# Two of four 31-tap convolution chunks taken off VectorE, six blocks ahead of the mixers' norm, and a last norm in smaller pieces

## The chip, the cores and the metric

The kernel runs on one core of a Trainium2 chip. The metric is the device time of one execution in microseconds (us), as the median of several. The engines are called by the names of the profile: PE is TensorE (PEld its weight loads), DVE is VectorE, ACT is ScalarE, POOL is GpSimd, and SP issues the DMAs.

## What is computed

A sequence of 256 tokens with 1024 features runs through two layers of a first block and two layers of a second block. The second block is where the change lies. A layer of it is: a SwiGLU feed-forward network (FFN), a layer norm, a mixer of three branches, a norm, a second FFN, a norm.

```python
h = layer_norm(ALPHA * h + 0.5 * swiglu(h, ffn1...), ln1)
mix = hybrid_mixer(h, ...)      # gated delta rule + convolution branch + latent attention, gated, @ w_out
h = layer_norm(ALPHA * h + mix, ln2)
h = layer_norm(ALPHA * h + 0.5 * swiglu(h, ffn2...), ln3)

def conv_branch(u, ...):
    h = u[..., :512] * sigmoid(u[..., 512:])
    h = causal_depthwise_conv(h, dw_w) + dw_b     # 31 taps, 512 channels
    h = silu(layer_norm(h, ln_g, ln_b))
    return h @ w_pw2 + b_pw2
```

## The kernel before

Activations lie with 128 features on the partitions and the 256 tokens along the free dimension, so a vector of 1024 features is eight chunks of 128x256. Weights come from memory in blocks of 128x1024 float32. Each block is split into a high part (`whi`, a copy on ACT) and a rest (`wlo`, a subtraction on DVE), and each product is three matmuls: high by high, high by low, low by high (`mm3`, L513). Eight PSUM banks (`ps`), twelve places for split weights (`spl`) and ten places for tiles of up to 288 columns (`t1`) are shared by all stages (`ROOM`, L1775).

The order of the work is not that of the program text. Every instruction is first recorded as an `Op` with a price (`price`, L277) and with what it must wait for. A planner (`run`, L305, and `schedule`, L318) lays the whole list out six times, backwards and forwards, picks the line with the earliest end by its prices, and the instructions are issued in that order. On the chip each engine runs its own instructions strictly in that order. All recorded instructions are issued from L409, so all rows of the profile have that line, and they are told apart by their tiles. The prices know each engine by itself; they have no term for two engines that hinder each other. A POOL operation on two tensors is priced at 0.154 us plus its columns by 480 per us.

The parts that the change touches, all in the second block:

- `taps_slow` (L1587) is one 128-channel chunk of the 31-tap convolution on DVE: one product with a bias, then 30 multiply-and-adds into the sum `cv`, each of 256 columns, reading `gluu` at a shifting offset. `conv_chunk` (L1574) calls it for each of four chunks in each of two layers. The four sums first meet in `conv_norm` (L1595), and what comes of that is used late in the mixer, with the weights `w_pw2`.
- `second_first` (L1213) says which weight blocks are multiplied with the not yet normed features (tiles `r`) while the norm's statistics are being worked out (`begin`, L574). Their results hold PSUM banks until the norm's factors are there, and are then mended on DVE by `fix` (L1176): a copy of two columns and two operations of 256 columns, `fx`. FFNs begin with six such blocks, mixers with four: `wi_krab` and three of `wi_dn`. All later blocks multiply the normed features (tiles `h`).
- `normed_begin` (L1103) holds `done`, which adds each result chunk to `x`, and `end` (L1152). For the last norm of the kernel, `end` multiplies all of `x` by one factor and adds another, in pieces of two chunks on DVE, then scales each chunk on ACT and stores it.
- `ffn` (L710) gives its results in two halves that `done` adds one after the other.

Other work that matters to the steps below: `delta` (L1356) and `unit_inverse` (L1482) are the gated delta rule, a long chain of small matmuls (`sm`) with DVE, ACT and POOL steps between them; the tile `NQ` is masked on POOL in it. `rsqrt` (L615) works out the norms' factor `rstd` on POOL.

Of the kernel before, what the change touches and what calls it, by code (L numbers as in the profile page):

```python
# [12 lines left out]
ACTF = mybir.ActivationFunctionType  # L13
# [3 lines left out]
P = 128  # L17
# [394 lines left out]
class Net:  # L412
# [294 lines left out]
            return Feat(norm, pss, fix)  # L707
        return take, end

    def ffn(self, F, wg, wu, wd, done, wide=False):  # L710

        a = self.halves("a", KF)
        for j in range(KF):
            g, gb = self.lin(wg[j], F, wide)
            u, ub = self.lin(wu[j], F, wide)
            sg = self.t([P, T], "sg")
            self.nc.scalar.activation(out=sg, in_=g, func=ACTF.Silu, **({} if gb is None else {"bias": gb}))
            av = self.t([P, T], "av")
            self.times(av, u, ub, sg)
            self.cut(a[j], av)  # L720
        for m in range(KD):
            ps = self.linear_f([w[m] for w in wd], a, True)
            done(m, ps[:, 0], ps[:, 1])

    def new_x(self):
        self.x = self.kept([P, KD, T], "x")
# [376 lines left out]
    def normed_begin(self, x, scale, gb, last=False):  # L1103


        nc = self.nc
        st = {}
        raw = []

        def sums(m):  # L1110
            if m == 0:
                st["s1"] = self.t([P, T], "s1")
                nc.vector.tensor_copy(out=st["s1"], in_=x[m])
            else:
                nc.vector.tensor_tensor(out=st["s1"], in0=st["s1"], in1=x[m], op=ALU.add)
            st["s2"] = self.add_square(st.get("s2"), x[m])
            if not last:
                self.cut_raw(raw[m], x[m], self.col(gb, 2 * m), self.col(gb, 2 * m, 2))

        def done(m, ps, ps2=None):  # L1120
            if ps2 is not None and m >= 4:
                nc.vector.tensor_tensor(out=x[m], in0=x[m], in1=ps2, op=ALU.add)
            if m < 4:
                nc.vector.scalar_tensor_tensor(out=x[m], in0=x[m], scalar=ALPHA / scale, in1=ps, op0=ALU.mult, op1=ALU.add)
            else:
                nc.vector.tensor_tensor(out=x[m], in0=x[m], in1=ps, op=ALU.add)
            if ps2 is not None and m < 4:
                nc.vector.tensor_tensor(out=x[m], in0=x[m], in1=ps2, op=ALU.add)
            if m == 1:
                st["s0"] = self.t([P, T], "s0")  # L1130
                nc.vector.tensor_tensor(out=st["s0"], in0=x[0], in1=x[1], op=ALU.add)
            if m == 2:
                ps0 = self.token_sums([st["s0"]])
                mu = st["mu"] = self.t([P, NT], "mu0")
                nc.vector.tensor_scalar(out=mu, in0=ps0[:, 0, :], scalar1=1.0 / 256, scalar2=None, op0=ALU.mult)
            if m == 3:
                pb = self.spread(st["mu"])
                if not last:
                    raw[:] = self.halves("r", KD, W)
                for k in range(4, KD):  # L1140
                    nc.vector.scalar_tensor_tensor(out=x[k], in0=x[k], scalar=ALPHA / scale, in1=pb, op0=ALU.mult,
                                                   op1=ALU.subtract)
                for k in range(4):
                    nc.vector.tensor_tensor(out=x[k], in0=x[k], in1=pb, op=ALU.subtract)
                for k in range(2):
                    sums(k)
            elif m > 3:
                if m < 6:
                    sums(m - 2)
                sums(m)  # L1150

        def end(first):  # L1152
            if last:
                for z, cols in zip((ALU.mult, ALU.add), self.moments(st["s1"], st["s2"], D, 1e-5 / scale ** 2)):
                    by = self.spread(cols).unsqueeze(1).to_broadcast([P, 2, T])
                    for m in range(0, KD, 2):
                        nc.vector.tensor_tensor(out=self.x[:, m:m + 2], in0=self.x[:, m:m + 2], in1=by, op=z)
                for m in range(KD):
                    nc.scalar.activation(out=x[m], in_=x[m], func=ACTF.Identity, scale=self.col(gb, 2 * m),
                                         bias=self.col(gb, 2 * m + 1))  # L1160
                    nc.sync.dma_start(out=self.out[m], in_=x[m])
                return None
            pss = self.begin(first, raw)
            rn = self.t([P, 2, T], "rn")
            nc.scalar.copy(out=rn, in_=self.spread2(*self.moments(st["s1"], st["s2"], D, 1e-5 / scale ** 2)))
            norm = self.halves("h", KD)
            for m in range(KD):
                w = self.t([P, T], "lnw")
                nc.scalar.activation(out=w, in_=rn[:, 1], func=ACTF.Identity, scale=self.col(gb, 2 * m),
                                     bias=self.col(gb, 2 * m + 1))  # L1170
                nc.vector.scalar_tensor_tensor(out=x[m], in0=x[m], scalar=self.col(gb, 2 * m), in1=rn[:, 0],
                                               op0=ALU.mult, op1=ALU.mult)
                nc.vector.tensor_tensor(out=x[m], in0=x[m], in1=w, op=ALU.add)
                self.cut(norm[m], x[m])

            def fix(ps, M):  # L1176
                c = self.t([P, 2], "fc")
                nc.vector.tensor_copy(out=c[0:M], in_=ps[:, T:W])
                o = self.t([P, T], "fx")
                nc.vector.tensor_tensor(out=o[0:M], in0=ps[:, 0:T], in1=rn[0:M, 0], op=ALU.mult)  # L1180
                nc.vector.scalar_tensor_tensor(out=o[0:M], in0=rn[0:M, 1], scalar=c[0:M, 0:1], in1=o[0:M],
                                               op0=ALU.mult, op1=ALU.add)
                return o[0:M], c[0:M, 1:2]
            return Feat(norm, pss, fix)
        return done, end
# [27 lines left out]
    def second_first(self, l, i):  # L1213
        ins = self.ins
        if i == 2:
            return [ins["wi_krab"][l]] + [ins["wi_dn"][l, j] for j in (4, 5, 6)]
        g, u = ins[f"f{(i + 1) // 2}g"][l], ins[f"f{(i + 1) // 2}u"][l]
        return [g[0], u[0], g[1], u[1], g[2], u[2]]

    def second_layer(self, l, x, F, last):  # L1220
        ins = self.ins
        for i in (1, 2, 3):
            end_all = last and i == 3
            done, end = self.normed_begin(x, 1.0 if i == 2 else 0.5, f"ln{i}{l}", end_all)
            if i == 2:
                self.hybrid(l, F, done)
            else:
                k = (i + 1) // 2
                self.ffn(F, ins[f"f{k}g"][l], ins[f"f{k}u"][l], [ins[f"f{k}d{j}"][l] for j in range(3)], done,
                         True)  # L1230
            if l == 0 and i == 3 and self.single:
                return end([])
            nl, ni = (l, i + 1) if i < 3 else (l + 1, 1)
# [340 lines left out]
    def conv_chunk(self, l, j, pa, pg, c, cs):  # L1574
# [7 lines left out]
        nc.vector.memset(u[:, 0:N], 0.0)  # L1582
        nc.vector.scalar_tensor_tensor(out=u[:, N:], in0=sg, scalar=1.0, in1=a, op0=ALU.add, op1=ALU.mult)
        cs.append(c)
        self.taps_slow(c, u, f"dw{l}_", 31, j, self.col(f"dw_b{l}", j))

    def taps_slow(self, out, src, name, n, ch, bias):  # L1587
        nc = self.nc
# [347 lines left out]
```

## Time and profile before

| | |
|---|---|
| time, median of 3 runs | 2287.04 us (2286.8 to 2287.19) |
| time of the profiled execution | 2288.66 us |
| its span in the profile | 2286.9 us |
| PE busy | 2249.1 us, 98% |
| PEld busy | 2103.8 us, 92% |
| DVE busy | 1858.2 us, 81% |
| ACT busy | 1288.8 us, 56% |
| POOL busy | 50.5 us, 2% |

The span is the time from the first to the last recorded instruction or transfer of one profiled execution; 1.8 us of that execution lie outside it, and that execution took 1.6 us more than the median. A matmul's end is modelled in the trace, so a busy PE is read together with what is marked as its idle time, and with the granted clock.

### The profile page before, as it was taken

The numbers are of one execution on the slowest core, as the hardware profiler recorded it, in microseconds if no ns is written. First come the engines' busy times: TensorE is split into PE (matmuls) and PEld (weight loads), VectorE is DVE, ScalarE is ACT, GpSimd is POOL, SyncE is SP. The second block draws the span as 40 slices with busy tenths as digits, with TensorE's granted clock in tenths as the row PEclk, the third lists the DMA queues.
The fourth block names the chain that finished last, engine by engine and source line by source line (L and its number), as shares of the span: only waits on it lengthen the run. The fifth ranks groups of instructions, "written<-read, shape, count | busy, mean of one in ns | idle before, by whom it ended". The sixth has DMA issues, their size and how long they took to land.

```text
span 2286.9 us, 41903 instructions
## 1 busy us (share of the span) xinstructions
PE 2249.1 (98%) x15948; PEld 2103.8 (92%) x15948; DVE 1858.2 (81%) x3690; ACT 1288.8 (56%) x2328; POOL 50.5 (2%) x46
## 2 busy tenths in 40 slices
PE   7999999999999999999999999999999999999997
PEld 6998899999989999888899999988988899999886
DVE  8888998798789755777789979977876899969865
ACT  4444765455445554466474756654664674656652
POOL 0000100000000000000001000000000010000000
PEclk9999999999999999999999999999999999999998
DMA  8999469888787555755542356555555441555652
GB/s 329 336 323 320 133 233 317 272 275 296 270 299 238 184 186 182 247 191 183 187 149 67 129 168 203 202 183 186 188 190 178 137 165 55 186 165 194 204 180 87
DMA packets 139788, 469.81 MB, mean 205 GB/s; under 512 B 15681, under 2 KB 20801, under 8 KB 139586
## 3 DMA queue, kind: packets, MB, share of 16 engines
q1 hardware_dynamic: 139586, 467.13, 60.6%
q8 instruction: 125, 2.05, 0.4%
q14 instruction: 77, 0.63, 0.1%
HBM read 466.02 MB, written 1.05 MB: 204 GB/s over the span
## 4 chain that ended last, share of the span: by engine, by line
PE 87%; DVE 5%; DMA 5%; ACT 1%; issue 1%; POOL 0%; ACTq 0%; SPq 0%; POOLq 0%; DVEq 0%
PE mm L409 82%; PE sm L409 5%; DMA raw<-in_ffn_wd_dram 2%; DVE wlo L409 1%; DVE raw L409 1%; DMA raw<-in_w_ada_dram 1%; ACT whi L409 1%; DMA raw<-in_ffn_wg_dram 1%; DVE x L409 1%; DVE cv__22491 L409 0%; DVE NQ L409 0%; DMA raw<-in_ffn_wu_dram 0%; DMA raw<-in_w_out_dram 0%; POOL rstd L409 0%; DVE cv__14517 L409 0%
## 5 line engine op out<-in xcount | busy, mean ns | idle before, releaser
L409 ACT CAST whi<-raw 128x1024 fp32r<-128x1024 f32 (+3 forms) x796 | 778.7, 982 | 590.9 <-PE mm L409 289.7
L409 DVE TENSOR_TENSOR wlo<-raw,whi 128x1024 fp32r<-128x1024 f32 (+3 forms) x796 | 901.6, 1137 | 240.0 <-PE mm L409 194.9
L409 DVE CUSTOM_DVE_ANT_0 raw<-raw,crep 128x1024 f32<-128x1024 f32 x144 | 175.0, 1219 | 36.2 <-DMA raw<-in_w_ada_dram 35.6
L409 ACT COPY half<-mm 128x256 f32<-128x256 f32 x158 | 57.7, 367 | 38.9 <-PE mm L409 37.4
L409 DVE TENSOR_TENSOR half<-mm,half 128x256 f32<-128x256 f32 x158 | 66.4, 420 | 16.0 <-ACT half L409 14.9
L409 POOL TENSOR_TENSOR rstd<-var,constt 128x2 f32<-128x2 f32 x18 | 18.3, 1017 | 1995.2 <-DVE var L409 1959.7
L409 ACT ACTIVATE sq<-x 128x256 f32<-128x256 f32 x96 | 38.6, 411 | 42.0 <-DVE x L409 39.7
L409 ACT ACTIVATE sg<-mm 128x256 f32<-128x256 f32 x79 | 30.1, 382 | 41.8 <-PE mm L409 37.3
L409 ACT ACTIVATE sg<-half 128x256 f32<-128x256 f32 x79 | 32.9, 418 | 27.3 <-DVE half L409 26.2
L409 DVE SCALAR_TENSOR_TENSOR x<-mm,gate,x 128x256 f32<-128x256 f32 x88 | 41.3, 478 | 7.6 <-PE mm L409 7.5
L409 DVE TENSOR_TENSOR sq<-sq 128x256 f32<-128x256 f32 x89 | 37.2, 418 | 4.0 <-ACT sq L409 3.7
L409 DVE TENSOR_TENSOR av<-mm,sg 128x256 f32<-128x256 f32 x79 | 33.1, 419 | 8.4 <-PE mm L409 8.1
L409 DVE TENSOR_TENSOR x<-x,mm 128x256 f32<-128x256 f32 x56 | 23.3, 416 | 17.0 <-PE mm L409 16.8
L409 DVE TENSOR_TENSOR av<-half,sg 128x256 f32<-128x256 f32 x79 | 33.3, 423 | 2.0
L409 DVE SCALAR_TENSOR_TENSOR dnc<-dnu,colt,dnc 128x256 f32<-128x256 f32 x72 | 31.7, 477 | 3.7 <-ACT dnc L409 3.6
L409 DVE SCALAR_TENSOR_TENSOR cv__22491<-gluu,colt,cv__22491 128x256 f32<-128x256 f32 x60 | 29.9, 514 | 0.0
L409 DVE SCALAR_TENSOR_TENSOR cv__14517<-gluu,colt,cv__14517 128x256 f32<-128x256 f32 x60 | 28.9, 506 | 0.0
L409 DVE SCALAR_TENSOR_TENSOR cv__15244<-gluu,colt,cv__15244 128x256 f32<-128x256 f32 x60 | 26.5, 474 | 0.0
L409 DVE SCALAR_TENSOR_TENSOR cv__23214<-gluu,colt,cv__23214 128x256 f32<-128x256 f32 x60 | 26.4, 475 | 0.0
L409 PEld LDWEIGHTS sm<-invX,NQ 128*128 128x128 f32 x192 | 23.7, 192 | 2.0 <-issue 1.4
L409 PE MATMUL sm<-invX,NQ 128*128 128x64 f32 x192 | 24.4, 271 | 0.9 <-DVE invX L409 0.9
L409 ACT COPY invX<-sm 128x256 f32<-128x256 f32 x20 | 7.6, 378 | 30.0 <-PE sm L409 26.6
(3361 smaller groups left out, 7993.9 us busy)
## 6 DMA issues: line engine op xcount, KB each, us to landing
raw<-in_w_ada_dram SPq DMA_DIRECT2D x144, 512.0 KB, 5.2
raw<-in_ffn_wg_dram SPq DMA_DIRECT2D x88, 512.0 KB, 5.1
raw<-in_ffn_wu_dram SPq DMA_DIRECT2D x88, 512.0 KB, 4.9
raw<-in_ffn_wd_dram SPq DMA_DIRECT2D x64, 512.0 KB, 5.0
raw<-in_wi_gate_dram SPq DMA_DIRECT2D x48, 512.0 KB, 3.2
raw<-in_f1g_dram SPq DMA_DIRECT2D x44, 512.0 KB, 3.8
raw<-in_f1u_dram SPq DMA_DIRECT2D x44, 512.0 KB, 4.1
raw<-in_f2g_dram SPq DMA_DIRECT2D x44, 512.0 KB, 4.4
```

The lines of the kernel that those rows point to most:

```text
L409: fn(*[real(a) for a in args], **{k: real(v) for k, v in kw.items()})
```

## The change

- Chunks 0 and 1 of the four convolution chunks go through a new function, `taps_apart`: ACT makes each of the 31 products (the first with the bias, straight into the sum; the others into a tile `tap`), and POOL adds the 30 others to the sum, one after the other. Chunks 2 and 3 stay on DVE.
- The mixers' list in `second_first` gets two more blocks of `wi_dn`, numbers 7 and 0, so that six blocks run ahead of the norm.
- In the last norm, both factors are spread first, and then each piece of `x` is multiplied and added to before the next one; the first two pieces are single chunks, the other three are pairs.
- In the last FFN, the last result chunk is accumulated in one half (three matmuls of 256 columns instead of one of 512 and one of 256), so that `done` adds it once.

```diff
-    def ffn(self, F, wg, wu, wd, done, wide=False):
+    def ffn(self, F, wg, wu, wd, done, wide=False, last=False):
...
         for m in range(KD):
-            ps = self.linear_f([w[m] for w in wd], a, True)
-            done(m, ps[:, 0], ps[:, 1])
+            ps = self.linear_f([w[m] for w in wd], a, not last or m < KD - 1)
+            done(m, *([ps] if last and m == KD - 1 else [ps[:, 0], ps[:, 1]]))
...
             if last:
-                for z, cols in zip((ALU.mult, ALU.add), self.moments(st["s1"], st["s2"], D, 1e-5 / scale ** 2)):
-                    by = self.spread(cols).unsqueeze(1).to_broadcast([P, 2, T])
-                    for m in range(0, KD, 2):
-                        nc.vector.tensor_tensor(out=self.x[:, m:m + 2], in0=self.x[:, m:m + 2], in1=by, op=z)
+                by = [self.spread(cols) for cols in self.moments(st["s1"], st["s2"], D, 1e-5 / scale ** 2)]
+                for m, n in ((0, 1), (1, 1), (2, 2), (4, 2), (6, 2)):
+                    for r, op in zip(by, (ALU.mult, ALU.add)):
+                        nc.vector.tensor_tensor(out=self.x[:, m:m + n], in0=self.x[:, m:m + n],
+                                                in1=r.unsqueeze(1).to_broadcast([P, n, T]), op=op)
...
         if i == 2:
-            return [ins["wi_krab"][l]] + [ins["wi_dn"][l, j] for j in (4, 5, 6)]
+            return [ins["wi_krab"][l]] + [ins["wi_dn"][l, j] for j in (4, 5, 6, 7, 0)]
...
-        self.taps_slow(c, u, f"dw{l}_", 31, j, self.col(f"dw_b{l}", j))
+        (self.taps_apart if j < 2 else self.taps_slow)(c, u, f"dw{l}_", 31, j, self.col(f"dw_b{l}", j))
+
+    def taps_apart(self, out, src, name, n, ch, bias):
+
+        nc = self.nc
+        nc.scalar.activation(out=out, in_=src[:, 0:T], func=ACTF.Identity, scale=self.col(f"{name}0", ch), bias=bias)
+        for i in range(1, n):
+            p = self.t([P, T], "tap")
+            nc.scalar.activation(out=p, in_=src[:, i:i + T], func=ACTF.Copy, scale=self.col(f"{name}{i}", ch))
+            nc.gpsimd.tensor_tensor(out=out, in0=out, in1=p, op=ALU.add)
```

## Rows read from the trace of the kernel before

**Rows 1.** Busy time, share of the span and instructions of each engine, whole kernel.

```profile
PE 2249.1 (98%) x15948; PEld 2103.8 (92%) x15948; DVE 1858.2 (81%) x3690; ACT 1288.8 (56%) x2328; POOL 50.5 (2%) x46
```

**Rows 2.** Stretch, length; busy of PE, PEld, DVE, ACT, POOL; granted clock; DMA share, GB/s.

```profile
1197.00:1256.00 59.00, 58.05 (x487) 57.08 (x487) 55.99 (x133) 29.04 (x70) 8.09 (x5) 1.00 0.23 74
```

**Rows 3.** The same stretch, DVE instructions that touch `gluu` alone: length, DVE busy.

```profile
1197.00:1256.00 59.00, 26.80 (x60) 1.00 0.23 74
```

**Rows 4.** Timeline of PE, mixers' beginnings: start, duration, instruction [idle before, releaser].

```profile
1151.96 0.43 PE L409 MATMUL sm<-constt,rstd 128*128 128x128 f32 x2 [0.50 <-POOL rstd L409]
1160.01 0.58 PE L409 MATMUL mm<-h__13933,whi 128*128 128x256 f32 x1 [2.62 <-DVE h__13933 L409]
...
1809.35 0.43 PE L409 MATMUL sm<-constt,rstd 128*128 128x128 f32 x2 [0.49 <-POOL rstd L409]
1824.64 0.61 PE L409 MATMUL sm<-constt,krab__22127 8*128 8x8 f32 x4 [1.75 <-ACT krab__22127 L409]
1826.71 0.44 PE L409 MATMUL sm<-constt,dn__22130 128*128 128x128 f32 x2 [1.10 <-ACT dn__22130 L409]
```

**Rows 5.** Stretches just behind those waits, columns as in rows 2.

```profile
1160.00:1200.00 40.00, 39.99 (x315) 39.84 (x316) 36.37 (x89) 31.79 (x78) 0.00 (x0) 0.93 0.50 159
...
1800.00:1840.00 40.00, 36.65 (x289) 35.71 (x288) 35.50 (x84) 29.78 (x71) 1.75 (x1) 0.96 0.39 135
```

**Rows 6.** A FFN's beginning with six early blocks, columns as in rows 2.

```profile
1414.00:1445.00 31.00, 31.00 (x262) 31.00 (x261) 29.74 (x68) 19.81 (x36) 1.55 (x1) 1.00 0.58 199
```

**Rows 7.** One tile, first mixer: duration in ns (least/median/most), first and last start.

```profile
L409 DVE TENSOR_TENSOR fx<-mm,rn x4: 410/414/414, 1158.5 to 1164.9; 128x256 f32<-128x256 f32 x3, 72x256 f32<-72x256 f32 x1
```

**Rows 8.** Groups by shape, DVE taps in the two mixers: count, busy us, mean ns.

```profile
L409 DVE SCALAR_TENSOR_TENSOR cv__14517<-gluu,colt,cv__14517 128x256 f32<-128x256 f32 x60 | 28.9, 506 | 0.0
...
L409 DVE SCALAR_TENSOR_TENSOR cv__15244<-gluu,colt,cv__15244 128x256 f32<-128x256 f32 x60 | 26.5, 474 | 0.0
...
L409 DVE SCALAR_TENSOR_TENSOR cv__22491<-gluu,colt,cv__22491 128x256 f32<-128x256 f32 x60 | 29.9, 514 | 0.0
```

**Rows 9.** One tile, ACT products with a per-partition factor: durations as in rows 7.

```profile
L409 ACT ACTIVATE dnc<-dnu,colt x24: 495/508/551, 1161.7 to 1853.4; 128x256 f32<-128x256 f32 x24
```

**Rows 10.** One tile each, POOL's operations (the memset from the groups, with mean).

```profile
L409 POOL TENSOR_TENSOR NQ<-NQ,constt x8: 1092/1269/2013, 1227.9 to 1893.1; 128x512 f32<-128x512 f32 x8
L409 POOL TENSOR_TENSOR rstd<-var,constt x18: 695/709/1747, 13.9 to 2276.2; 128x2 f32<-128x2 f32 x18
L409 POOL MEMSET rope__67<- 64x256 f32 x2 | 0.6, 305 | 0.3 <-POOLq L1925 0.3
```

**Rows 11.** Timeline of POOL and DVE where both work, columns as in rows 4.

```profile
1227.93 2.33 POOL L409 TENSOR_TENSOR NQ<-NQ,constt 128x512 f32<-128x512 f32 x2 [11.23 <-DVE NQ L409]
1228.16 1.15 DVE L409 SCALAR_TENSOR_TENSOR cv__14517<-gluu,colt,cv__14517 128x256 f32<-128x256 f32 x1
...
1807.53 1.22 DVE L409 TENSOR_TENSOR wlo<-raw,whi 128x1024 fp32r<-128x1024 f32 x1
1807.55 1.75 POOL L409 TENSOR_TENSOR rstd<-var,constt 128x2 f32<-128x2 f32 x1 [186.17 <-DVE var L409]
```

**Rows 12.** Timeline of PE in the delta rule's chain, columns as in rows 4.

```profile
1234.14 1.08 PE L409 MATMUL sm<-invX,NQ 128*128 128x64 f32 x8 [0.93 <-DVE invX L409]
...
1896.67 0.55 PE L409 MATMUL sm<-invW,invY 128*128 128x64 f32 x3 [1.15 <-DVE invW L409]
```

**Rows 13.** Timeline of the kernel's last 15 us, columns as in rows 4.

```profile
2272.43 0.88 DVE L409 TENSOR_TENSOR x<-x,mm 128x256 f32<-128x256 f32 x2 [5.93 <-PE mm L409]
...
2277.68 1.88 DVE L409 TENSOR_TENSOR x<-x,sm 128x512 f32<-128x512 f32 x3 [0.59 <-PE sm L409]
2278.88 3.67 DVE L409 TENSOR_TENSOR x<-x,sm 128x512 f32<-128x512 f32 x6
2279.66 2.29 ACT L409 ACTIVATE x<-x,colt 128x256 f32<-128x256 f32 x4 [5.90 <-DVE x L409]
...
2282.05 2.07 ACT L409 ACTIVATE x<-x,colt 128x256 f32<-128x256 f32 x4
```

## What the change was predicted to do

> **What bounds the kernel now.** I began with the engines' busy times: PE is busy 2249.1 of 2286.9 us, DVE 81%, POOL 2% [rows 1]. The matmuls that the change leaves as they are fill the span, so an edit can only win time in which PE waits or runs at a lower clock. Next came the stretches: where the first mixer's convolution lies, DVE is busy 55.99 of 59 us, but PE 58.05 of the same 59 [rows 2]. DVE is full there because the planner fills its gaps with taps, which nobody waits for. Taps take 26.80 of the 55.99 [rows 3]. Last I read PE's timeline for waits in the three places that the diff touches: the mixers' beginnings [rows 4], the delta rule [rows 12] and the end [rows 13].
>
> **Six early blocks.** At the first mixer PE waits 0.50 us for the norm's factor and then 2.62 us for the first normed chunk `h`; at the second 0.49 us for the factor, 1.75 for `krab` and 1.10 for the first `dn` chunk [rows 4]. After each of these waits the granted clock is lower: 0.93 as a mean over 40 us and 0.96 [rows 5], so PE ran part of them at 1.2 instead of 2.4 GHz. That cost 40 x 0.07 = 2.8 and 40 x 0.04 = 1.6 us. The waits for `h`, `krab` and `dn` are 5.5 us, the clock 4.4, together 9.9; the two waits for the factor, 1.0 us more, come from POOL, which the edit leaves alone.
>
> Two more early blocks are work for PE that needs no normed chunk. A block is 8 x 3 = 24 matmuls; 262 of them, most of this size, take 31 us at the FFN's beginning [rows 6], so a block is some 2.8 us and two are 5.7 us, more than the longest wait. The cost is two more mendings on DVE, of two operations near 0.41 us and a small copy [rows 7]: about 2 us a layer, beside PE's 5.7. What is late next is the mendings themselves: `krab` is one of six and not of four. I leave half of its wait (0.9 us) standing and take -9.0 us, with the bounds -9.9 and 0. The weights of the two blocks are only issued earlier on SP's queue, behind the same 12 places. The nearest evidence that six are enough is that at an FFN, with six early blocks and the same norm, PE is busy 31.00 of 31.00 us at a clock of 1.00 [rows 6].
>
> **Taps on ACT and POOL.** Off DVE go 60 multiply-and-adds a layer, which hold it 26.5 us where nothing hinders them [rows 8]. As PE waits for DVE only here and there, this relief is worth at most the waits in the delta rule's chain, 0.93 and 1.15 us [rows 12]. ACT gets 62 products a layer, each at most 0.51 us [rows 9], 31 us; it is idle 59 - 29 = 30 us in the stretch [rows 2] and more behind it. So ACT holds them only if they spread over the whole stretch, some 1 us apart.
>
> POOL gets 60 adds a layer. No row has one of 256 columns. The bounds are a memset of 256 columns that reads nothing, 0.305 us, and a product of 512 columns, 1.09 us at the least [rows 10]. The latter is nearest in kind; half of it is 0.55, and a fixed part speaks for somewhat more, so I take 0.65: 60 x 0.65 = 39 us a layer (18 to 65). The sums are wanted late, so this time is off the path by itself.
>
> What is on it is that POOL and DVE hinder each other. A tap started while POOL masks `NQ` takes 1.15 us instead of 0.47, and `rstd`, 0.70 us alone, takes 1.75 when a `wlo` runs beside it [rows 10, 11]. The 60 taps that met the masks took 28.9 us against 26.5 for the other pair, 2.4 us more; in the second layer 29.9, so 3.4 more [rows 8]. There are four masks a layer of some 1.27 us [rows 10], 5.1 us. So 0.47 to 0.67 of POOL's time returns as time of DVE: of 39 us some 18 to 26. That nearly eats the 26.5 us that leave. DVE's load stays about what it is, and so PE need not slow down as a whole. But the planner knows nothing of it, and each engine keeps its planned order: a `wlo`, or a step of the delta chain, stands behind a blocked operation on DVE, the masks of `NQ` stand behind adds on POOL, and copies for the chain stand on ACT behind a product that waits for a `tap` place. Both present waits, 0.93 and 1.15 us, lie where masks run [rows 11, 12]. I take it that the adds cost twice that again, 2 x 2.1 = +4.2 us, with bounds of -2.1 (both vanish) and +26 (below).
>
> The Trainium skill, page "SBUF — State Buffer", section "Who interferes with whom", has a rule that speaks against this change: a DVE instruction with two SBUF inputs contends with a GpSimd instruction that reads SBUF, and whichever comes second waits for the whole of the first. The rows agree (1.15 instead of 0.47 us). By that rule the adds would not run beside DVE's tensor work but between it; that is the second case below.
>
> **The end.** One add of 0.44 us goes from the path behind the last matmul [rows 13]. DVE now applies the factors from 2277.68 to 2282.55, eight operations of 0.61, and ACT ends at 2284.12 [rows 13]. In pieces there are four operations of 0.34 to 0.44 us and six of 0.61, 5.0 to 5.4 us, so DVE ends at 2282.7 to 2283.1; only two ACT operations of 0.52 follow, to 2283.7 to 2284.1. That is 0 to 0.4 us more. I take -0.6 in all (-0.4 to -0.9). The single-half last result passes the same columns through PE; I cost it at nothing.
>
> **The sum.** -9.0 + 4.2 - 0.6 = -5.4 us. These are differences, read in an execution of 2288.66 us; I set them against the median, 2287.04, since a wait of a few tenths is the same in both: 2281.6 us, and 2276 to 2286 with the smaller of the bounds.
>
> **Rivals.**
>
> - *The adds hold up the plan.* Slower. In the stretch DVE has 29 us of other work and, if the planner pulls the other two chunks' taps forward, 53; with POOL's 39 and its present 8 that is 100 us in 59. Then DVE runs 18 to 26 us a layer behind its plan. Of the delays at the masks, PE saw 0.93 of 2.4 and 1.15 of 3.4 us, a good third [rows 8, 12]; that gives 7 to 9 us a layer, and 13 if PE sees half of 26. The sum is -9.6 + 16 = +6 us, 2293, and up to 2304 with 26. It decides from 4.8 us of new waiting a layer, 0.08 us of PE per add. For it: the rows on hindrance [rows 11] and the full DVE [rows 2]. Against it: 26.5 us of filler leave DVE's queue, so fewer instructions stand ahead of a chain step.
> - *The relief is real.* The adds fall where DVE has no tensor pair to read, or are nearer the lower bound of 18 us; the chain's waits go too. -9.9 - 2.1 - 1.0 (the waits for the factor) - 0.9 = -14 us: 2273. Against it: the wait for the factor comes from POOL and `wlo`, which stay.
> - *Six blocks bring nothing.* Six results and two banks for the norm's sums and factors fill all eight PSUM banks, so PE stops as late as before until the first mending, and the DVE work of 2 us a layer comes on top. 0 to +4 for the beginnings, +4.2, -0.6: about 2291, or the time of before if the adds cost little. Against it: the FFNs' beginnings have the same banks.
>
> **How the numbers follow.** Chances: the forecast 0.45, the plan held up 0.29, real relief 0.11, nothing from six blocks 0.15. A measurement of this kernel tells about 0.2%, 4.6 us, from no change, so faster means below 2282.5 and slower above 2291.6. Of the forecast's chance 0.34 lies below, 0.10 within, 0.01 above; of the held-up plan 0.27 above and 0.02 within; real relief is below; of the last case 0.02, 0.06 and 0.07. That makes faster 0.47, same 0.18, slower 0.35. Cases of both signs hold most of the chance, so the range is wider than the forecast's own 2276 to 2286: it goes from real relief, 2273, to most of the held-up plan, 2302, and leaves out about 0.15.
>
> **What would show it.** Right: no idle PE and a clock of 1.00 in the 40 us behind both mixer norms; adds near 0.65 us at their least, with a mean well above; DVE taps and `wlo` in the convolution's stretch longer than 0.47 and 1.2 us; PE's waits in the delta rule grown by about 2 us a layer. The forecast falls if PE's waits there pass 4.8 us a layer, if ACT is found waiting for POOL (a `tap` place) ahead of a `whi`, or if PE still stands idle behind the mixers' norms.

## The result: 58 us slower

The changed kernel takes 2345.19 us (median of 4 runs, 2343.55 to 2347.93) beside 2286.92 us for the kernel before in the same series: a ratio of 1.0257, 95% interval 1.0245 to 1.0269, or 58.3 us more. I had forecast 2281.6 us and a range up to 2302. The profiled execution has a span of 2342.7 us, 55.8 us more than that of before.

The page of the changed kernel, busy times and two rows of its forty equal slices, to be held beside [rows 1]:

```profile
PE 2280.5 (97%) x15970; PEld 2128.7 (91%) x15970; DVE 1852.6 (79%) x3579; ACT 1347.1 (58%) x2457; POOL 160.3 (7%) x166
...
POOL 0000100000000000000064000000000063000000
PEclk9999999999999999999997999999999999999999
```

DVE has 111 instructions fewer and yet only 5.6 us less to do. PE has 22 more but 31.4 us more busy time: nearly the same work at a lower clock. Nearly all of POOL's work lies in four slices, in the two mixers. Where the loss lies is seen in 40 us stretches of the changed kernel (columns: the stretch and its length, busy us and instructions of each engine, PE's granted clock, DMA share, GB/s):

```profile
core 0: us, PE busy (x) PEld busy (x) DVE busy (x) ACT busy (x) POOL busy (x), PEclk, DMA share, GB/s
1160.00:1200.00 40.00, 35.23 (x278) 34.05 (x277) 34.45 (x63) 31.36 (x83) 11.42 (x11) 0.96 0.49 163
1200.00:1240.00 40.00, 32.89 (x240) 31.03 (x239) 29.89 (x54) 31.31 (x65) 35.17 (x34) 0.91 0.29 96
1240.00:1280.00 40.00, 35.92 (x201) 32.80 (x199) 33.88 (x71) 26.82 (x61) 22.27 (x24) 0.76 0.03 11
1280.00:1320.00 40.00, 40.00 (x252) 37.75 (x252) 30.80 (x80) 18.05 (x57) 2.02 (x2) 0.78 0.17 56
1840.00:1880.00 40.00, 35.44 (x274) 34.32 (x273) 36.17 (x87) 32.26 (x86) 0.70 (x1) 0.91 0.39 128
1880.00:1920.00 40.00, 32.94 (x272) 32.26 (x270) 27.56 (x42) 31.59 (x66) 37.58 (x40) 0.95 0.41 138
1920.00:1960.00 40.00, 34.00 (x213) 30.99 (x214) 37.43 (x75) 31.39 (x67) 23.19 (x27) 0.84 0.09 25
```

In these 280 us PE is idle 280 - 246.4 = 33.6 us. What the clock takes I estimate as PE's busy time times one less the granted clock, row by row: 32.1 us (31.8 if each mixer's stretch is taken as a whole). Together that is 65.7 us. The kernel before has 2.4 us of idle time and, by stretches as wholes, 3.2 us of clock there, so by this estimate 60 us more are lost here, against 58.3 measured: half as waiting, half as clock. The clock falls behind the waiting. PE stood idle 7.1 us in 1200:1240 and 4.1 us in 1240:1280; 1280:1320, in which PE is busy throughout, still has a mean of 0.78. In stretches of 10 us the level itself can be read (columns as above):

```profile
1260.00:1270.00 10.00, 8.64 (x45) 8.03 (x43) 9.52 (x16) 6.04 (x18) 9.17 (x12) 0.69 0.02 2
1270.00:1280.00 10.00, 10.00 (x46) 9.71 (x45) 5.77 (x15) 3.00 (x9) 1.26 (x2) 0.50 0.06 20
1280.00:1290.00 10.00, 10.00 (x41) 9.41 (x41) 5.18 (x12) 1.25 (x3) 0.00 (x0) 0.50 0.05 13
1290.00:1300.00 10.00, 10.00 (x50) 9.23 (x49) 6.35 (x16) 1.63 (x4) 0.00 (x0) 0.60 0.00 0
1300.00:1310.00 10.00, 10.00 (x81) 9.17 (x80) 9.51 (x24) 6.15 (x16) 0.00 (x0) 1.00 0.10 28
```

From 1270 to 1290 PE runs at 0.50, which is 1.2 GHz, without a gap in its work; from 1300 on it runs at 2.4 GHz again.

The groups that the change added, and the short convolution's taps `dnc` that stayed on DVE (busy us, mean ns; after the second bar the idle time ahead of them and what ended it):

```profile
L409 POOL TENSOR_TENSOR cv__14372<-cv__14372,tap 128x256 f32<-128x256 f32 x60 | 58.2, 991 | 45.1 <-ACT tap L409 43.5
L409 ACT ACTIVATE tap<-gluu,colt 128x256 f32<-128x256 f32 x120 | 56.9, 506 | 22.8 <-POOL cv__14372 L409 8.6 <-POOL cv__22541 L409 5.9 <-PE sm L409 3.8
L409 POOL TENSOR_TENSOR cv__22541<-cv__22541,tap 128x256 f32<-128x256 f32 x60 | 51.8, 886 | 54.5 <-ACT tap L409 53.7
L409 DVE SCALAR_TENSOR_TENSOR dnc<-dnu,colt,dnc 128x256 f32<-128x256 f32 x72 | 38.1, 556 | 6.8 <-ACT dnc L409 6.6
```

An add takes 0.89 to 0.99 us on the mean where the planner counts 0.69, and `dnc` takes 0.56 us in the place of the 0.48 of before. The shortest and the median add of each layer, from the view of a tile (ns, minimum, median, maximum; start of the first and the last):

```profile
L409 POOL TENSOR_TENSOR cv__14372<-cv__14372,tap x60: 717/804/1772, 1187.8 to 1270.6; 128x256 f32<-128x256 f32 x60
L409 POOL TENSOR_TENSOR cv__22541<-cv__22541,tap x60: 721/737/1767, 1880.1 to 1957.7; 128x256 f32<-128x256 f32 x60
```

Even the shortest, 0.72 us, is over the plan. The timeline of POOL in the first mixer shows what lateness means:

```profile
1187.79 30.98 POOL L409 TENSOR_TENSOR cv__14372<-cv__14372,tap 128x256 f32<-128x256 f32 x30 [37.77 <-ACT tap L409]
1218.74 2.90 POOL L409 TENSOR_TENSOR rqk<-rqk,constt 128x16 f32<-128x16 f32 x1
1221.62 11.34 POOL L409 TENSOR_TENSOR cv__14372<-cv__14372,tap 128x256 f32<-128x256 f32 x10
...
1242.04 0.73 POOL L409 TENSOR_TENSOR cv__14372<-cv__14372,tap 128x256 f32<-128x256 f32 x1 [0.77 <-ACT tap L409]
...
1247.64 1.09 POOL L409 TENSOR_TENSOR NQ<-NQ,constt 128x512 f32<-128x512 f32 x1 [4.88 <-DVE NQ L409]
```

Thirty adds take 31 us where the plan has 30 x 0.69 = 21, and `rqk`, the first step of the delta rule on POOL, stands behind them. The first `NQ` starts at 1247.6; before, it started at 1227.93 [rows 11]. DVE, in the same mixer, shows the other half, the hindrance (start, length; the small ones have 8 columns):

```profile
1212.67 1.76 DVE L409 TENSOR_TENSOR wlo<-raw,whi 128x1024 fp32r<-128x1024 f32 x1
...
1218.10 0.70 DVE L409 TENSOR_SCALAR spd<-spe 128x8 f32<-128x8 f32 x1
1218.84 0.20 DVE L409 RECIPROCAL spd<-spd 128x8 f32<-128x8 f32 x1
1219.08 0.17 DVE L409 TENSOR_TENSOR sps<-spe,spd 128x8 f32<-128x8 f32 x1
...
1226.45 0.69 DVE L409 TENSOR_TENSOR brk<-rqk,beta 128x8 f32<-128x8 f32 x1
```

While adds run, this `wlo` takes 1.76 us and not the 1.22 of [rows 11], and small operations that take 0.17 us take 0.70. It is one of the longest: the 19 `wlo` of this width that lie beside adds for four fifths of their time or more take 1.21 to 1.77 us, with a median of 1.65.

### The profile page after: what moved, and what is told of

Its sections match the earlier page's. It is cut to its first block, busy times and chain, and to the rows that moved or that the text cites. A ratio compares the mean times of both kernels' runs of the same rounds, so it can differ in the third digit from the quotient of the medians.

```text
span 2342.7 us, 42185 instructions
## 1 busy us (share of the span) xinstructions
PE 2280.5 (97%) x15970; PEld 2128.7 (91%) x15970; DVE 1852.6 (79%) x3579; ACT 1347.1 (58%) x2457; POOL 160.3 (7%) x166
## 4 chain that ended last, share of the span: by engine, by line
PE 85%; DVE 5%; DMA 3%; POOL 2%; ACT 2%; issue 2%; SPq 0%; POOLq 0%; ACTq 0%; DVEq 0%
PE mm L409 80%; PE sm L409 5%; DVE wlo L409 1%; POOL cv__14372 L409 1%; POOL cv__22541 L409 1%; DMA raw<-in_w_ada_dram 1%; DVE x L409 1%; ACT whi L409 1%; DMA raw<-in_ffn_wd_dram 1%; DMA raw<-in_ffn_wg_dram 1%; DVE raw L409 1%; DVE NQ L409 0%; DMA raw<-in_w_out_dram 0%; DMA raw<-in_ffn_wu_dram 0%; POOL rqk L409 0%
## 5 line engine op out<-in xcount | busy, mean ns | idle before, releaser
L409 ACT ACTIVATE tap<-gluu,colt 128x256 f32<-128x256 f32 x120 | 56.9, 506 | 22.8 <-POOL cv__14372 L409 8.6
L409 POOL TENSOR_TENSOR cv__14372<-cv__14372,tap 128x256 f32<-128x256 f32 x60 | 58.2, 991 | 45.1 <-ACT tap L409 43.5
L409 POOL TENSOR_TENSOR cv__22541<-cv__22541,tap 128x256 f32<-128x256 f32 x60 | 51.8, 886 | 54.5 <-ACT tap L409 53.7
L409 ACT ACTIVATE sg<-half 128x256 f32<-128x256 f32 x79 | 32.8, 418 | 26.3 <-DVE half L409 24.1
L409 DVE SCALAR_TENSOR_TENSOR dnc<-dnu,colt,dnc 128x256 f32<-128x256 f32 x72 | 38.1, 556 | 6.8 <-ACT dnc L409 6.6
L409 DVE TENSOR_TENSOR x<-x,mm 128x256 f32<-128x256 f32 x55 | 22.9, 416 | 16.4 <-PE mm L409 16.2
L409 PEld LDWEIGHTS sm<-invX,NQ 128*128 128x128 f32 x192 | 31.2, 244 | 1.7 <-PE sm L409 0.4
L409 PE MATMUL sm<-invX,NQ 128*128 128x64 f32 x192 | 31.6, 326 | 0.6 <-DVE invX L409 0.3
L409 DVE SCALAR_TENSOR_TENSOR cv__15018<-gluu,colt,cv__15018 128x256 f32<-128x256 f32 x60 | 30.2, 518 | 0.4
```

The source lines that it names most:

```text
L409: fn(*[real(a) for a in args], **{k: real(v) for k, v in kw.items()})
```

## Experiments

Fifteen kernels are to tell apart the parts of the change and the two suspects: POOL being late against the plan, and POOL's reads holding up DVE. The table sums them up. "Difference" is the median less that of the kernel before in the same series; "idle" and "clock" are PE's idle time and the clock's estimated cost in 1160 to 1320 and 1840 to 1960 us, each stretch taken as a whole; "DVE" is DVE's busy time over the whole profiled span.

| kernel | add planned | in the add's place | difference, us | ratio, 95% | idle + clock, us | DVE, us |
|---|---|---|---|---|---|---|
| before | | | | | 2.4 + 3.2 | 1858.2 |
| e1_six | no adds | | -2.9 | 0.9981 to 0.9998 | 2.8 + 0 | 1860.5 |
| e2_end | no adds | | +0.8 | 0.9998 to 1.0016 | 2.7 + 1.6 | 1857.9 |
| e3_taps | 0.69 | add | +35.6 | 1.0140 to 1.0171 | 21.6 + 17.0 | 1846.6 |
| e4_act_dve | on DVE | add on DVE | +1.6 | 1.0008 to 1.0057 | 5.3 + 1.6 | 1852.8 |
| after | 0.69 | add | +58.3 | 1.0245 to 1.0269 | 33.6 + 31.8 | 1852.6 |
| e6_noread | 0.69 | two memsets | +16.2 | 1.0057 to 1.0087 | 11.0 + 6.5 | 1820.3 |
| e7_noread_long | 0.69 | three memsets | +48.6 | 1.0172 to 1.0226 | 28.8 + 27.0 | 1821.2 |
| e8_places | 0.69 | add | +57.0 | 1.0233 to 1.0264 | 26.3 + 33.6 | 1857.8 |
| e5_priced | 0.97 | add | +30.5 | 1.0117 to 1.0148 | 22.4 + 12.1 | 1856.2 |
| e9_priced_noread | 0.97 | three memsets | +2.0 | 1.0001 to 1.0020 | 6.2 + 3.1 | 1820.4 |
| e11_price_more | 1.30 | add | +29.2 | 1.0110 to 1.0144 | 23.3 + 14.2 | 1854.9 |
| e13_tell_dve | 0.97 | add | +29.1 | 1.0113 to 1.0144 | 26.7 + 7.6 | 1864.2 |
| e14_one_read | 0.97 | one operand read | +6.8 | 1.0019 to 1.0043 | 8.8 + 4.6 | 1827.5 |
| e10_masks | 0.69 | add | +51.7 | 1.0180 to 1.0249 | 30.5 + 32.8 | 1854.3 |
| e12_one | 0.69 | add, half as many | +26.5 | 1.0082 to 1.0143 | 13.2 + 10.0 | 1855.3 |
| e15_taps_priced | 0.97 | add | +32.2 | 1.0122 to 1.0156 | 22.1 + 14.8 | 1855.4 |

The column of idle time and clock follows the measured difference to within 5 us once the 5.6 us of before are taken off, in all rows but e10 (6 us over) and e12 (9 us under), whose executions differ by 18 and 15 us among themselves. So in these kernels, too, the loss is in the two stretches.

### The parts alone

**Six early blocks.** The edit of `second_first` alone:

```diff
-            return [ins["wi_krab"][l]] + [ins["wi_dn"][l, j] for j in (4, 5, 6)]
+            return [ins["wi_krab"][l]] + [ins["wi_dn"][l, j] for j in (4, 5, 6, 7, 0)]
```

> The kernel before with the six early blocks alone; the taps stay on DVE and the end stays as it was. If the six blocks do what the prediction said of them, this is 7 to 10 us faster than before (2277 to 2280). If they bring nothing, it is within 2 us of before. If they themselves cause part of the 58 us, it is slower by more than 5 us.

It took 2283.61 us beside 2286.54, 2.9 us less. PE's waits at the two beginnings in this kernel (total us, times, longest), to be held beside [rows 4]:

```profile
PE mm L409 <- DVE h__13921 L409: 1.0, 1, 1.0
PE sm L409 <- POOL rstd L409: 0.5, 1, 0.5
...
PE sm L409 <- ACT krab__22119 L409: 1.3, 1, 1.3
PE sm L409 <- ACT dn__22138 L409: 1.2, 2, 0.8
PE sm L409 <- ACT dn__22105 L409: 0.6, 2, 0.4
```

At the first mixer the wait for `h` fell from 2.62 to 1.0 us and the clock of 1160 to 1200 rose from 0.93 to 1.00. At the second, `krab` still costs 1.3 and the `dn` chunks 1.8 us, 3.1 in the place of 2.85: the wait is for mending, and there is more to mend. The clock of 1800 to 1840 stays at 0.96. So there is a small gain, between 0.5 and 4.3 us by the interval, and its middle is a third of what I took.

**The end.** The loop of the last norm and the single half, alone:

```diff
+                by = [self.spread(cols) for cols in self.moments(st["s1"], st["s2"], D, 1e-5 / scale ** 2)]
+                for m, n in ((0, 1), (1, 1), (2, 2), (4, 2), (6, 2)):
```

> The kernel before with the last norm in smaller pieces and the single-half last result alone. Prediction: 0.4 to 0.9 us faster, since one DVE add leaves the path behind the last matmul. Rival: no difference beyond 0.2 us either way.

No difference that can be told. The end of the changed kernel, to be held beside [rows 13]:

```profile
2328.28 0.42 DVE L409 TENSOR_TENSOR x<-x,mm 128x256 f32<-128x256 f32 x1 [6.06 <-PE mm L409]
...
2333.07 5.69 DVE L409 TENSOR_TENSOR x<-x,sm 128x256 f32<-128x256 f32 x10 [0.59 <-PE sm L409]
...
2338.86 1.09 ACT L409 ACTIVATE x<-x,colt 128x256 f32<-128x256 f32 x2 [0.23 <-DVE x L409]
```

One add of 0.44 us is gone, the ten pieces take 5.69 us where eight took 4.87 (2277.68 to 2282.55) and ACT ends 1.2 us behind the last piece where it ended 1.6 us behind it. From the first add to the end of the span it is 14.4 us, and it was 14.5.

**The taps alone, and the same with the sums on DVE.** The second has the edit's ACT half without its POOL half:

```diff
-            nc.gpsimd.tensor_tensor(out=out, in0=out, in1=p, op=ALU.add)
+            nc.vector.tensor_tensor(out=out, in0=out, in1=p, op=ALU.add)
```

> The kernel before with the taps of chunks 0 and 1 on ACT and POOL alone. Theory: this part holds all of the loss, and the loss is larger than 58 us by what the other two parts win, so 2345 to 2356 us. Rival: the loss comes from the taps and the six early blocks together (both load DVE, ACT and the small tiles at the mixer's start); then this is clearly under 2335 us.

> As the taps alone, with the products on ACT, but the 30 sums of a chunk on DVE in place of POOL. DVE then has as many operations as before (an add in place of each multiply-and-add). If POOL is the cause, by hindering DVE or by its queue, the loss goes: within 6 us of before. If ACT is the cause (62 products a layer ahead of copies that the delta chain waits for), most of the loss stays: more than 25 us slower.

With POOL 35.6 us are lost, without it 1.6 by the median. The expectation for the taps alone missed: it had 2345 or more, and the rival came, so the six blocks and the taps lose together some 25 us that neither loses alone. Of the ten executions with the sums on DVE seven took 2286 to 2291 us and three 2306 to 2308, at a mean clock of 0.987 and not 0.994 to 0.996; no trace of these three was kept, and what made them slower isn't shown. In the other seven ACT's 62 products a layer, their `tap` places and their distance from the casts `whi` cost next to nothing; the loss of the taps is POOL's.

### Late against the plan, or in DVE's way

The next two keep the order of the changed kernel on every engine, instruction for instruction, and put memsets of the product's tile where the adds were, two or three for each (`range(2)` or `range(3)`); a memset only writes and doesn't read, and the sums of chunks 0 and 1 are left out. The price stays 0.69.

```diff
-            nc.gpsimd.tensor_tensor(out=out, in0=out, in1=p, op=ALU.add)
+            with nc.together():
+                for _ in range(2):
+                    op = nc.gpsimd.memset(p, 0.0)
+            op.cost = 0.154 + T / 480.0
+            nc.touch(op, out, True)
```

> The changed kernel with its planned order kept on every engine, but each of the 120 adds on POOL is replaced by two memsets of the tap tile (256 columns each, about 0.31 us in the kernel before, so some 0.65 us a pair, near the planner's price of 0.69). The sums of chunks 0 and 1 are left out. POOL's queue, the places of the taps and ACT's products stay as they are, but POOL reads no SBUF. If POOL and DVE hindering each other is the cause, directly or by making POOL late, the loss goes: 2280 to 2292 us. If the cause is the queue on POOL as such (the delta rule's operations behind 30 adds) or ACT's 62 products a layer, most of the loss stays: above 2325 us.

> As the run with two memsets, with three in place of each add: some 0.95 us, as long as the adds took on the chip (mean 0.89 to 0.99), in the same planned order. POOL is then as late against its plan as in the changed kernel, but reads no SBUF and so holds up no DVE instruction. If DVE's being blocked is the cause, this stays under 2295 us. If POOL's lateness is the cause (the planner thought 0.69 us; ACT waits for a tap place, and the delta rule's POOL operations come late), this is above 2320 us. In between, both count, in proportion.

Two memsets of 0.31 us are inside the planned 0.69, three are not: in the fence below ninety take 29.97 us, 1.0 for each add. That alone, with no read on POOL, takes the loss from 16.2 to 48.6 us (39 to 52 by the interval). DVE's busy time is the same in both (1820.3 and 1821.2 us), so it isn't hindered; it waits. POOL and DVE with three memsets:

```profile
1189.71 29.97 POOL L409 MEMSET tap<- 128x256 f32 x90 [37.75 <-ACT tap L409]
1219.65 2.92 POOL L409 TENSOR_TENSOR rqk<-rqk,constt 128x16 f32<-128x16 f32 x1
```

```profile
1908.47 0.76 DVE L409 SCALAR_TENSOR_TENSOR spq<-spq,spu 128x8 f32<-128x8 f32 x4
...
1913.62 0.42 DVE L409 TENSOR_TENSOR rt<-sin,sm 128x256 f32<-128x256 f32 x1 [2.19 <-POOL tap L409]
```

`rqk` is as late as with adds. The second fence shows a place that I had thought of for ACT alone: `rt` on DVE needs one of the ten `t1` places, and the one it was given holds a product that POOL has not yet taken. PE waits 5.5 us for that `rt`. In the changed kernel the same wait is PE's longest; there POOL isn't what `rt` waits for, and it comes behind a row of blocked small operations and a `wlo` (DVE, then PE):

```profile
1913.31 1.38 DVE L409 SCALAR_TENSOR_TENSOR spq<-spq,spu 128x8 f32<-128x8 f32 x2
...
1915.41 1.74 DVE L409 SCALAR_TENSOR_TENSOR spq<-spq,spu 128x8 f32<-128x8 f32 x4
...
1919.65 0.41 DVE L409 TENSOR_TENSOR rt<-sin,sm 128x256 f32<-128x256 f32 x1
```

```profile
1920.21 0.66 PE L409 MATMUL sm<-constt,dnv 128*128 128x128 f32 x2 [7.16 <-DVE rt L409]
```

Four of the `spq` steps take 1.74 us here and 0.76 us beside memsets. So either suspect alone makes the same wait long: POOL's lateness beside memsets, the blocked steps beside adds. The 16.2 us with two memsets lie between the two outcomes expected (within 6 us, or 39 and more): a part of the loss needs no reads and next to no lateness, for thirty pairs of memsets take 22 us where the plan has 21.

**The right price.** The changed kernel with `op.cost = 0.97` for the add, and the same with three memsets in the add's place:

> The changed kernel with the planner's price of each add raised from 0.69 to 0.97 us, its mean on the chip; nothing else differs but the order that follows. If a wrong price for POOL is what spoils the order, the loss shrinks to under 10 us (below 2297). If the loss comes from DVE's being blocked, which no price of POOL tells the planner, more than 30 us stay (above 2317).

> The changed kernel with the add planned at 0.97 us, and in the place of each add three memsets of the product's tile (0.31 us each in the trace of the run with three memsets, so 0.95 us an add); the sums of chunks 0 and 1 are left out. The priced kernel with real adds lost 30 us against the kernel before. If what remained there is the reading of the two operands (VectorE held back), this run falls to the 16 us of the run with two memsets or below: 2300 to 2303. If it is the order that the plan makes round a GpSimd that holds the chain for 30 us and more, it stays at 2310 to 2317.

The price alone gives back 27.8 of 58.3 us, which leaves 30.5, at the lower edge of the second outcome expected. Without the reads all but 2.0 are back, with POOL about as long at work (158.2 us busy; 170.2 with adds at the same price, 160.3 in the changed kernel). That is the cleanest pair of the study: the same order on every engine, adds of 1.04 and 0.98 us on the mean against three memsets that take 1.0 with their gaps, and 28.5 us between them. The pages' busy times, with memsets and with adds (e9, then e5):

```profile
PE 2248.6 (98%) x15970; PEld 2104.0 (92%) x15970; DVE 1820.4 (80%) x3579; ACT 1339.2 (59%) x2455; POOL 158.2 (7%) x406
```

```profile
PE 2262.5 (98%) x15970; PEld 2112.7 (91%) x15970; DVE 1856.2 (80%) x3579; ACT 1342.0 (58%) x2455; POOL 170.2 (7%) x166
```

The same 3579 DVE instructions take 35.8 us longer beside the adds.

**Is that 28 us lateness too?** The add planned at 1.30 us, above all means seen, and then the add at 0.97 with DVE's remaining taps planned at 0.49 and not 0.40 us:

```diff
-            nc.vector.scalar_tensor_tensor(out=out, in0=src[:, i:i + T], scalar=self.col(f"{name}{i}", ch),
+            op = nc.vector.scalar_tensor_tensor(out=out, in0=src[:, i:i + T], scalar=self.col(f"{name}{i}", ch),
                                            in1=out, op0=ALU.mult, op1=ALU.add)
+            op.cost = 0.49
```

> The changed kernel with the add planned at 1.30 us, above all that the traces show of it on the mean (0.99). If lateness against the plan is the cause, nothing is late now and less is lost than with 0.97: 10 to 25 us, 2297 to 2312. If what 0.97 left is the price of an order that waits for a long GpSimd chain, planning it longer gives no less: 30 to 45 us, 2317 to 2332.

> The changed kernel with the add planned at 0.97 us and each tap that stays on VectorE (convolution and short convolution, 128x256) planned at 0.49 us in the place of the 0.40 that the planner's formula gives; the traces show 0.46 to 0.47 without adds and 0.55 beside them. If what is left of the loss (30 us with the price alone) is VectorE being late against the plan, 15 us or more of it come back: under 2302. If the time is lost because VectorE really works longer, or because each blocked small operation stands in the chain, it stays at 2310 to 2320.

29.2 and 29.1 us: nothing comes back. No price that I gave POOL or the taps buys off the reads. But the taps are a small part of what the reads hold up: between e9 and e5 `dnc` and `cv` on DVE grow by 9.5 of the 35.8 us. The `wlo` and the small steps kept their old prices, so that DVE's lateness against the plan is the way in which the reads cost PE time isn't excluded.

**One operand.** Each add replaced by an operation that reads the product alone:

```diff
-            op = nc.gpsimd.tensor_tensor(out=out, in0=out, in1=p, op=ALU.add)
+            op = nc.gpsimd.tensor_scalar(out=out, in0=p, scalar1=1.0, scalar2=None, op0=ALU.mult)
```

> The changed kernel with the add planned at 0.97 us, and each add replaced by an operation of GpSimd that reads the product alone, multiplies it by one and writes it over the sum; the sums of chunks 0 and 1 are left out. If one operand read is enough to hold VectorE, and the operation takes as long as the add, the loss stays near 30 us: 2310 to 2320. If the loss needs two operands read, or follows the length of the operation and that is shorter, it falls to 0 to 12 us: 2285 to 2299. The length in the trace tells these last two apart by the taps' mean on VectorE (0.46 us if it isn't held, 0.50 and more if it is).

The operation is longer than the add, and the loss is 6.8 us. Its group, and a `wlo` that runs while 37 of these operations follow one another on POOL without a gap:

```profile
L409 POOL TENSOR_SCALAR cv__14252<-tap 128x256 f32<-128x256 f32 x60 | 64.6, 1094 | 32.9 <-ACT tap L409 31.5
```

```profile
1176.92 42.87 POOL L409 TENSOR_SCALAR cv__14252<-tap 128x256 f32<-128x256 f32 x37 [27.13 <-ACT tap L409]
```

```profile
1209.88 1.21 DVE L409 TENSOR_TENSOR wlo<-raw,whi 128x1024 fp32r<-128x1024 f32 x1
1211.01 0.76 DVE L409 SCALAR_TENSOR_TENSOR spq<-spq,spu 128x8 f32<-128x8 f32 x3
1211.69 0.48 DVE L409 SCALAR_TENSOR_TENSOR dnc<-dnu,colt,dnc 128x256 f32<-128x256 f32 x1
```

This `wlo` and `dnc` have their free lengths, 1.21 and 0.48 us, and of all 30 `wlo` that lie beside such operations the median is 1.22 and the longest 1.44. The smallest are held a little: `spq` steps take 0.24 us on the mean, beside memsets 0.17 and beside adds 0.41. So nearly all of the hindrance goes with the second operand, or with this kind of operation: one that reads two operands and isn't an add, or one operand at another rate, wasn't tried.

### Which queue carries it

**Own places for the products** (eight, of a kind of their own, so that they take none of the ten):

```diff
-            p = self.t([P, T], "tap")
+            p = nc.spot("tp", [P, T], F32, "tap")
```

> The changed kernel with eight places of their own for the tap tiles, in place of the ten that they share with all small tiles. If ACT standing behind POOL for a place is a main cause, the loss shrinks by more than 20 us (below 2325). If DVE's being blocked is the cause, it moves by less than 10 us.

Nothing is gained, but the plan is another, and it teaches something: `rqk` comes ahead of all adds.

```profile
1198.49 2.90 POOL L409 TENSOR_TENSOR rqk<-rqk,constt 128x16 f32<-128x16 f32 x1 [48.34 <-PE mm L409]
1214.60 11.89 POOL L409 TENSOR_TENSOR cv__14769<-cv__14769,tap 128x256 f32<-128x256 f32 x11 [13.21 <-ACT tap L409]
```

PE then waits for DVE: in the first mixer 4.2 us for `gm`, 2.7 for `invW`, 2.5 for `invX`, in the second 8.9 for one `gm`. The changed kernel itself has only two adds ahead of `rqk` in its second mixer, and loses 28 us of idle time and clock there:

```profile
1880.07 1.56 POOL L409 TENSOR_TENSOR cv__22541<-cv__22541,tap 128x256 f32<-128x256 f32 x2 [38.02 <-ACT tap L409]
1881.74 2.91 POOL L409 TENSOR_TENSOR rqk<-rqk,constt 128x16 f32<-128x16 f32 x1
```

So `rqk` behind thirty adds is how the loss looks in one mixer of one plan and not its cause.

**The delta rule's masks on DVE** (the two operations on `NQ` moved from POOL, with `rqk` left there):

> The changed kernel with the delta rule's two masks for each half (the operations on NQ) on VectorE in the place of GpSimd, so that they no longer queue behind the adds; rqk stays on GpSimd. If the masks queued behind the adds carry the loss, 25 us or more of the 58 come back: 2320 or less. If the loss hangs on rqk and on the sums themselves being late for all that follows them, under 10 us come back: 2335 to 2350 (the masks cost VectorE about 1 us each).

6.6 us come back of 58.3, by the interval 1 to 17; one of the four executions took 2322.75 us, the others 2338 to 2340. The masks' place behind the adds is a small part, less than a third at the most.

**One chunk of four**, `j < 1` in the place of `j < 2`:

> The changed kernel with one chunk of four on ScalarE and GpSimd (30 adds a layer in the place of 60). If each late add costs its share, half of the 58 us is lost: about 2316. If the loss begins only where GpSimd is late beyond the slack that the plan has, little is lost: 2284 to 2295, and the relief of VectorE could show as a gain: 2275 to 2284.

Half of the adds cost 26.5 us, a little under half. Thirty a layer aren't free; fewer weren't tried.

**The taps alone at the right price:**

> The taps alone (no six early blocks, no other end), with the add planned at 0.97 us. If the six blocks matter only through the wrong price, this loses what the changed kernel loses with the right price, 25 to 35 us: 2312 to 2322. If the six blocks bring load to the place where the adds run whatever the price, it loses clearly less: 5 to 20 us, 2292 to 2307.

32.2 us, beside 35.6 at 0.69. So the price matters little without the six blocks. If the reads cost there what they cost in the changed kernel (28.5 us), they make up nearly all of the loss; the taps alone without reads weren't run. With the six blocks the wrong price costs 28 us more. In the taps alone 24 adds stand ahead of the first mixer's `rqk`, in the changed kernel 30; in the second mixer it is 3 and 2. Whether the six blocks cause this, or only another plan came out, isn't settled.

## Why the prediction was wrong, step by step

**What bounds the kernel** held: what the kernels lose or win lies in PE's waits and its clock, and those lie in the two mixers. But I read DVE as full of "filler that nobody waits for", and so a slower DVE as nearly free. That reading failed. The adds held up `wlo`, `dnc`, `spq` and `gm` too: with the right price PE waits 2.8 us for `wlo` and 2.7 for `invX` in the two mixers beside adds, and 0.4 for each beside memsets. The signs that I named against the forecast showed: PE stands idle 15 and 16 us longer in the two mixers than before, where my limit was 4.8 for the delta rule; ACT waits 14.5 us for POOL ahead of its products; and PE still stands idle 4.6 us for `dn` behind the first mixer's norm.

**Six early blocks, -9.0 us: mis-sized, -2.9 measured.** The clock came back at the first mixer as worked out (0.93 to 1.00), and at the second it stayed at 0.96. The wait at the second did not go: the mending of six results took its place. That was among the things I named as late next, and I left it 0.9 us where 3.1 stand.

**The add's length, 0.65 us: too short.** It is 0.72 us at the least and 0.89 to 0.99 on the mean. Half a mask of 512 columns was the wrong way to halve. It makes 52 to 58 us a layer and not 39, within the bounds of 18 to 65. The step that I didn't take was to hold it against the planner's price of 0.69 and multiply by the adds in a row: 0.3 us of error on thirty adds is 10 us of lateness, and each engine keeps its order. With reads excluded, the length beyond the price takes the loss from 16.2 to 48.6 us.

**"The sums are wanted late, so this time is off the path by itself": wrong.** The sums are, but POOL's queue isn't, nor are the `t1` places that the products hold. `rqk` waits in the one, `rt` on DVE for the other.

**DVE's delay, 18 to 26 us a layer: nearly right, by luck.** It is 35.8 us in the two layers between the kernels with the right price (e5 against e9), and 31.4 in the changed kernel against three memsets: 16 to 18 a layer, at the lower end or just under it. But two errors offset each other. The share of POOL's time that returns on DVE is 0.3 (35.8 of 121 us of adds, 31.4 of 110) and not 0.47 to 0.67, and POOL's time is 52 to 62 us a layer and not 39. The Trainium skill, page "SBUF — State Buffer", section "Who interferes with whom", has a DVE instruction with two SBUF inputs contend with a GpSimd instruction that reads SBUF. The trace agrees for GpSimd reading two operands (one `wlo` 1.76 us for 1.22). For the operation of GpSimd that reads one it shows next to nothing of it (`wlo` 1.21 us).

**What PE makes of it, +4.2 us: the step that failed most.** I carried over the share that PE saw of four masks a layer, and took twice that. The reads alone cost 28.5 us where the plan is right, 0.8 of DVE's 35.8, and not a third. My reading, which no run tests, is that a mask falls between two steps of one chain, while sixty adds lie beside everything that DVE does for some 80 us. Nor did I count the clock behind the waits for this step, though I had for the first: of the 60 us found in the stretches, 29 are clock.

**The end, -0.6 us:** it is +0.8, not to be told from 0. The pieces took 5.69 us and not 5.0 to 5.4, which ate the 0.44 saved.

**The rivals.** "The adds hold up the plan" had the place, the sign and the point of decision, and its upper price, 13 us a layer, is nearly what the reads cost with the right price (14). That is luck as well: it took half of 26 us, and the runs show 0.8 of 18. It priced the hindrance and forgot that POOL itself is late. That is why even its 2304 falls short by 41 us. Two figures beside it don't come out of their terms: 29 us of other work and 26.5 of taps are 55.5 and not 53, and the bounds given don't make 2276 to 2286. Neither decides anything. I had the wrong one likeliest because I let 26.5 us of relief on DVE stand against 18 to 26 us of delay, as if both were filler.

**What stays open.** The order planned at 0.69 costs 16.2 us even when POOL keeps to it and reads nothing, and that planned at 0.97 costs 2.0. The `dn` waits at the mixers' beginnings are a large part of it: with two memsets PE waits 4.6 us for `dn` at the first and 4.8 at the second, with the order planned at 0.97 and memsets 0 and 1.8, and 2.1 for `h`. Why the first order has them I haven't found. The shares can't be added up either: reading costs some 10 us on top of lateness (58.3 against 48.6) and 28.5 without it.

Of all these kernels only the one with the six blocks alone is faster than before, by 2.9 us, and that is less than the 0.2% that I called a difference. Its interval ends at 0.9998.

## What to carry to other kernels

Before work is moved to an idle engine, hold the new operation's length against the price that the plan has for it and multiply by the instructions in a row: an order made beforehand turned 0.3 us of error on each add into tens of us here, on what shares the queue or the places. Then ask what the new engine reads while the old one works; busy time that moves from DVE to POOL came back on DVE as 0.3 us for each add. And count the clock behind each wait: here it doubled the price of the waiting.

## What of the hardware was not expected

- POOL adding two tensors of 128x256 takes 0.72 us at the least and 0.89 to 1.04 us on the mean in these kernels. Meanwhile a `wlo` on DVE takes up to 1.77 us for 1.22 in the changed kernel (median 1.65), and operations of 8 columns 0.65 to 0.70 us for 0.17.
- POOL reading one operand of the same size, 1.06 to 1.09 us an operation, leaves `wlo` at a median of 1.22 us, and DVE's total within 7.1 us of that beside memsets (1827.5 and 1820.4). With two operands it is 35.8 us more.
- A memset of 128x256 on POOL takes 0.31 us and leaves `wlo` at 1.23 us.
- Behind 11.2 us of idle time (1200 to 1280 of the changed kernel) PE's granted clock was 0.50, or 1.2 GHz, for 20 us in which PE was busy throughout (1270 to 1290), and 1.00 again from 1300 on.
